# A static planner's stated durations and the order of a delta-rule mixer's projections, in a kernel of three blocks on one Trainium2 core

## The chip, the cores and the metric

The kernel runs on one core of one Trainium2 chip. The metric is the device time of one execution in microseconds. A core has five engines that run their own instruction streams in order and wait for each other by semaphores: TensorE (PE, matrix products and transposes), VectorE (DVE), ScalarE (ACT), GpSimd (POOL) and SyncE (SP, which here only issues DMAs). TensorE writes to PSUM, which has eight banks of 128 x 512 float32.

## The reference, cut to what matters

The sequence has 512 tokens of width 1024, in float32. Layer 0 is a dilated band attention with a memory attention and a SwiGLU of width 2816. Layer 1 is a gated delta-rule mixer (DeltaNet) with a memory attention and again a SwiGLU. A second block with three mixers of its own (gated linear attention, S5, sparse attention) follows. The change touches the order of work in layer 1's mixer, and the planner that orders everything. The mixer, cut:

```python
qkv, z, gate_in, q_mem = split(h @ w_in, ...)          # 3*768, 768, 24, 256 columns
q, k, v = split(silu(conv5(qkv)), 3)                   # 6 heads of 128
q, k = l2norm(q) * 128 ** -0.5, l2norm(k)
g, beta = -exp(a_log) * softplus(gate_in[..., 0] + dt_bias), sigmoid(gate_in[..., 1])
# forward and backward, per head, in chunks of tokens:
decay = exp(tril(g_i - g_j))                           # g: running sum in the chunk
a     = strict_tril(k_beta @ k.T * decay) + eye
u, w  = triangular_solve(a, [v * beta, k_beta * exp(g)])   # the inverse
intra = tril(q @ k.T * decay)
# then chunk by chunk a state S: v_new = u - w S; out = (q exp(g)) S + intra v_new; S = S exp(g_last) + ...
o = (o_fwd + o_bwd) normed * out_norm * silu(z)
out = concat([o, memory_attention(q_mem)]) @ w_out
```

## The kernel before

**Products in three passes.** Each float32 operand is split into a high and a low part (`wh`, `wl` for weights, `Xh`, `Xl` for activations), and `mm3` (lines 271 to 273) issues three matmuls into one bank: high by low, low by high, high by high. A projection of 128 columns over 512 tokens is eight `mm3` of 128x128 by 128x512. Weights come in pieces of 512 KB: `fetch` issues the DMA on SP into one of three raw buffers, `high` rounds the piece on ACT (line 243, two halves), `low` subtracts on DVE (line 262, two halves).

**The planner.** `Flow` builds the program by list scheduling. Each part of the work is a Python generator that yields an engine and a stated cost before it issues an instruction, or a wait for an event, or a request for a buffer (`get`, one of a counted set). `run` keeps a modelled clock per engine, picks the engine whose next step could start first, and among the steps of that engine that could start within `DELTA` = 0.1 us takes the one with the smallest `late`. The step then occupies its engine for its cost, and its result is ready at the end of it; a step on another engine can start `HOP` = 0.2 us after that. The result is a fixed order of instructions per engine. The costs do nothing else: no instruction waits for a planned time. Stated costs are `act(n)` = 0.1 + 0.00084 n (0.1 more with an accumulator or a per-partition scale), `dve(n)` = 0.07 + 0.00105 n, 0.65 us for an `mm3` of 512 columns and 0.33 us for one of 256 in most places, 0.68 us in `tok_proj`.

**The mixer.** In `deltanet` (line 1168) every head has threads `key`, `decays`, `query`, `value`, `gate`, `inverse`, two of `chain` (forward and backward), and `gate_out`.

- `key` takes the projection from its bank, convolves (ACT copy line 1313, DVE taps line 1322), normalises, transposes to `ktok` and `kTh`, multiplies `kk` (line 1392) and copies it to `kkn`.
- `decays` makes, for each direction d, a row broadcast `rowbc` (line 279), the decay `AT`, and from `kkn` and `AT` the matrix `Ln` (line 1424, DVE). It takes a bank of the set `px` for each d, and asks for the second one after d = 0 is done, which needs `kkn`.
- `query` multiplies `kq` (line 1447) and holds a `px` bank until `AT` of both directions is there.
- `inverse` waits for both `Ln` and then goes through six levels and a last half level: products and transposes on PE (`x`, lines 1508 and 1512), ACT copies (line 1519), products on PE (`y`, line 1533), DVE predicated copies (line 1537). At the end PE line 1553, DVE copies (line 1558) and ACT (line 1546) write `Uf`. Two inverses can be in flight.
- `chain` then walks over four chunks (lines 1580 to 1616), and each of the two chains of a head holds a `px` bank from its start to its end.
- `gate_out` norms, transposes and writes `oT`, which `splits` rounds for the output projection.

The banks are counted in sets: `mm` 2, `px` 3, `lv` 3. Other sets that bind here: `E` 2 (raw keys, values and gates), `qT` 1, `Ln`, `AT`, `qe`, `kd`, `k` 2 each. `projector` (line 1775) is the thread that issues the projections, in the order of a list, with `late` = 20, so that each `mm3` of it fills PE where nothing else is ready. The first four of the list run in two halves of 256 columns and on two lent banks. A projection holds its `mm` bank until its consumer has copied it out. The same list orders the DMAs and the splits of the weights.

**The list before** (`deltanet_weights`, line 1158): gates, then for heads 0, 1, 2 key, query, value, z; then the memory's two; then key, query, value of heads 3, 4, 5; then z of heads 3, 4, 5.

Of the kernel before, what the change touches and what calls it, by code (L numbers as in the profile page):

```python
# [35 lines left out]
S = 512  # L36
# [19 lines left out]
class Flow:  # L56
# [4 lines left out]


    HOP = 0.2

    def __init__(self, **sets):
        self.free = dict.fromkeys(("PE", "ACT", "DVE", "POOL", "DMA"), 0.0)
# [32 lines left out]
    def run(self):  # L99
        while self.threads:  # L100
            again = True
            while again:
                again = False
                for t in list(self.threads):
                    kind, *arg = t["req"]
                    value = None
                    if kind == "get" and any(self.sets[n] for n in arg):
                        value = min((n for n in arg if self.sets[n]), key=lambda n: min(self.sets[n])[0])
                        tok = min(self.sets[value])
                        self.sets[value].remove(tok)  # L110
                    elif kind == "two" and len(self.sets[arg[0]]) > 1:
                        for _ in range(2):
                            tok = min(self.sets[arg[0]])
                            self.sets[arg[0]].remove(tok)
                    elif kind == "wait" and all(e["tok"] for e in arg):
                        tok = max((e["tok"] for e in arg), key=lambda x: x[0])
                    elif kind == "move" and self.sets[arg[0]]:
                        src, dst = arg
                        tok = min(self.sets[src])
                        self.sets[src].remove(tok)  # L120
                        self.put(dst, tok)
                        tok = t["tok"]
                    elif kind == "late":
                        t["late"] = arg[0]
                        tok = t["tok"]
                    else:
                        continue
                    if tok[0] > t["tok"][0]:
                        t["tok"] = tok
                    self.step(t, value or tok)  # L130
                    again = True
            ops = []
            for t in self.threads:
                if t["req"][0] in self.free:
                    eng, cost, *after = t["req"]
                    ops.append((self.start(eng, after or [t["tok"]]), t))
            assert ops or not self.threads, ([(t["gen"].__name__, t["req"]) for t in self.threads], self.sets, self.free)
            if not ops:
                return
            s, t = min(ops, key=lambda x: x[0])  # L140
            s, t = min((x for x in ops if x[1]["req"][0] == t["req"][0] and x[0] <= s + DELTA), key=lambda x: x[1]["late"])
            eng, cost = t["req"][:2]
            self.free[eng] = s + cost
            t["tok"] = (s + cost, eng)
            self.step(t, t["tok"])
# [17 lines left out]
class K:  # L163
# [132 lines left out]
    def inputs(self, F, W, eX, eM, eF, pro):  # L296
# [93 lines left out]
        def memory():  # L390
            yield "late", 0.5
            for l in range(2):
                yield "wait", *eN[l]
                for c in range(2):
                    ev = W["mk"][l][c]
                    yield "wait", ev
                    yield "get", "mm"
                    p = self.psum("mm")
                    w = ev["W"]
                    for k in range(KT):  # L400
                        t = yield "PE", 0.33
                        self.mm3(p[:, :256], (w.h[:, k, :], w.l[:, k, :]), (M[l].h[:, k, :], M[l].l[:, k, :]),
                                 k == 0, k == KT - 1)
                    F.put("wsl", t)
                    F.add(evac(self.memK[l][:, c, :], p), 0.5, t)
                yield "wait", *W["mv"][l]
                for u in range(2):
                    yield "get", "mm"
                    p = self.psum("mm")
                    ts = slice(u * P, (u + 1) * P)  # L410
                    for k in range(KT):
                        w, kk = W["mv"][l][k // 4]["W"], k % 4
                        t = yield "PE", 0.33
                        self.mm3(p[:, :256], (M[l].h[:, k, ts], M[l].l[:, k, ts]), (w.h[:, kk, :], w.l[:, kk, :]),
                                 k == 0, k == KT - 1)
                    F.add(evac(self.memV[l][:, u, :], p, l == 1 and u == 1), 0.5, t)
                for _ in range(2):
                    F.put("wsl", t)
# [118 lines left out]
    def attention(self, F, W, eX, eM, eB, at, e2):  # L537
# [41 lines left out]
        def group(g):  # L579
# [37 lines left out]
            for i, t0 in enumerate((0, 64, 192, 320, 384)):  # L617
                yield "get", "mm"
                p = self.psum("mm")
                for k in range(KT):  # L620
                    w, kk = W2[k // 4]["W"], k % 4
                    t = yield "PE", 0.33
                    self.mm3(p[:, :256], (X.h[:, k, t0:t0 + P], X.l[:, k, t0:t0 + P]), (w.h[:, kk, :], w.l[:, kk, :]),
                             k == 0, k == KT - 1)
                F.add(copy_v(g, i, p[:, :256], r["t"][2][:, i, :], "mm"), g - 0.5, t)
# [394 lines left out]
    def out_ffn(self, F, i, W, gnext, groups, kev, before):  # L1020
# [57 lines left out]
        for part, (f0, f1) in enumerate(self.PARTS):  # L1078
# [22 lines left out]
            while f < nf:  # L1101
                fs = (f, f + 1) if part == 0 and f == 0 else (f,)
                banks = {}
                for hv in ((0, 256), (256, 512)) if len(fs) == 2 else ((0, 512),):
                    t0, t1 = hv
                    for u in range(t0 // P, t1 // P):
                        yield "wait", eX[u]
                    for f_ in fs:
                        for z in range(2):
                            ev = gu[part][f_][z]  # L1110
                            yield "wait", ev
                            if (f_, z) not in banks:
                                nm = yield "get", *self.ANY
                                banks[f_, z] = self.psum("bk"), nm
                            p = banks[f_, z][0]
                            for k in range(KT):
                                tk = yield "PE", 0.65 * (t1 - t0) / 512
                                self.mm3(p[:, t0:t1], (ev["W"].h[:, k, :], ev["W"].l[:, k, :]),
                                         (X.h[:, k, t0:t1], X.l[:, k, t0:t1]), k == 0, k == KT - 1)
                            if t1 == S:  # L1120
                                F.put("wsl", tk)
                        if t1 == S:
                            F.add(evac_gu(f_, (banks[f_, 0], banks[f_, 1], tk)))
                f += len(fs)
                if part == 0 and f == 4:
                    yield "DMA", 1.4
                    r["post"], _ = row("rowA", a["norm_ffn_post"][i])
                    yield "DMA", 1.4
                    r["gain"], _ = row("rowB", gnext)
                    r["ev"] = [F.event() for _ in range(4)]  # L1130
                    r["eX"] = [F.event() for _ in range(4)]
                    r["store"] = True
                    n4[:] = [0] * 4
# [24 lines left out]
    def deltanet_weights(self):  # L1158
# [2 lines left out]
        r = {n: [self.weight(w, 0, KT, z * 768 + h * P, P) for h in range(6)] for z, n in enumerate("qkvz")}  # L1161
        r["g"] = self.weight(w, 0, KT, 3072, P)
        r["m"] = [self.weight(w, 0, KT, 3096 + c * P, P) for c in range(2)]
        N = 3
        heads = [[r[n][h] for n in ("kqvz" if h < N else "kqv")] for h in range(6)]
        return r, [r["g"]] + sum(heads[:3], []) + r["m"] + sum(heads[3:], []) + r["z"][N:]

    def deltanet(self, F, wev, order, eX, res):

# [587 lines left out]
    def proj(self, F, ev, eX, m=P):  # L1757
# [7 lines left out]
        for t0, t1 in rngs:  # L1765
            yield "wait", *eX[t0 // P:t1 // P]
            for k in range(KT):
                t = yield "PE", 0.65 * (t1 - t0) / S
                self.mm3(p[:m, t0:t1], (W.h[:, k, :], W.l[:, k, :]), (X.h[:, k, t0:t1], X.l[:, k, t0:t1]),
                         k == 0, k == KT - 1)  # L1770
        F.put("wsl", t)
# [3 lines left out]
    def projector(self, F, items, eX, eP, late=20, haste=0):  # L1775
# [9 lines left out]
        def part(it, t0, t1):  # L1785
            W, m = it["W"], it["args"][4]
            yield "wait", *eX[t0 // P:t1 // P]
            for k in range(KT):
                t = yield "PE", 0.65 * (t1 - t0) / S
                self.mm3(it["p"][:m, t0:t1], (W.h[:, k, :], W.l[:, k, :]), (X.h[:, k, t0:t1], X.l[:, k, t0:t1]),  # L1790
                         k == 0, k == KT - 1)
            if t1 == S:
# [13 lines left out]
        for i, it in enumerate(items):  # L1806
# [13 lines left out]
            for u in range(4):  # L1820
# [3 lines left out]
                sl = slice(u * P, (u + 1) * P)  # L1824
                for k in range(KT):
                    W, kk = it[k // 4]["W"], k % 4
                    t = yield "PE", 0.33
                    self.mm3(p[:, :256], (X.h[:, k, sl], X.l[:, k, sl]), (W.h[:, kk, :], W.l[:, kk, :]),
                             k == 0, k == KT - 1)
                evac, late_ = it[0]["use"]["f"]  # L1830
# [392 lines left out]
    def s5(self, F, W, eX, open_, eY, uT):  # L2223
# [140 lines left out]
        def glu():  # L2364
# [14 lines left out]
            for c in range(2):  # L2379
                zs = []  # L2380
                for o in (2, 0):
# [1 line left out]
                    p = self.psum("lv", "glu")  # L2383
                    os_ = slice((o + c) * P, (o + c + 1) * P)
                    for k in range(2):
                        t = yield "PE", 0.65
                        self.mm3(p, (w.h[:, k, os_], w.l[:, k, os_]), yh[k], k == 0, k == 1)
                    zs.append((p, t))
                if c:
# [896 lines left out]
```

## Time and profile before

| what | value |
|---|---|
| time, median of 3 runs (lowest to highest) | 1768.99 us (1767.22 to 1770.46) |
| time of the profiled execution | 1771.96 us |
| its span, first to last instruction | 1770.2 us |
| mean granted clock of TensorE over the span | 0.99 of full speed |

The sum of a prediction is made against the profiled execution, 1771.96 us, of which 1.8 us lie around its span; it is 3.0 us over the median of the runs. Layer 1's mixer fills about 660 to 1020 us of the span.

### The profile page before, as it was taken

The page shows a single profiled execution, that of the slowest core. Times are in us where ns is not written, and L with a number is a line of the kernel's source. Part 1 is how long each engine was busy: PE and PEld are TensorE (multiplying, and loading weights), DVE is VectorE, ACT ScalarE, POOL GpSimd, SP SyncE. Part 2 cuts the span into 40 slices and gives each one's busy share as a digit, 9 for nine tenths or more (in the row PEclk, how much of TensorE's full clock was granted, in tenths as well). Part 3 has the DMA queues.
Part 4 walks back from the last instruction along what each step waited for, and adds up shares of the span by engine and source line. Part 5 has one row for each costly group of instructions (what it writes and reads, how often), then busy time and mean ns, then how long its engine had stood idle before and what let it go on. Part 6 is the DMA issues. An engine that isn't in the chain of part 4 may idle for free.

```text
span 1770.2 us, 30809 instructions
## 1 busy us (share of the span) xinstructions
PE 1718.8 (97%) x12391; PEld 1431.1 (81%) x12391; DVE 951.0 (54%) x1895; ACT 797.4 (45%) x1922; POOL 276.0 (16%) x440
## 2 busy tenths in 40 slices
PE   6999999999999999999999899999999999999999
PEld 5988679888888887787877778888888888888787
DVE  6333656323333378756765467464433468467573
ACT  5443635333222247657666455333222353345671
POOL 5200001000000020000000152375540033210000
PEclk8999999999999999999999999999999999999999
DMA  6513133333233333102010165344333253552012
GB/s 194 152 51 96 49 119 96 119 96 95 96 95 96 96 119 84 50 26 61 26 49 26 33 157 141 104 146 134 106 108 102 80 154 112 151 160 70 25 37 84
DMA packets 211983, 167.88 MB, mean 95 GB/s; under 512 B 21996, under 2 KB 183036, under 8 KB 211840
## 3 DMA queue, kind: packets, MB, share of 16 engines
q1 hardware_dynamic: 203808, 154.39, 29.6%
q0 software_dynamic: 4560, 9.42, 2.1%
q10 hardware_dynamic: 3472, 2.10, 0.4%
q8 instruction: 97, 1.59, 0.4%
q14 instruction: 46, 0.38, 0.1%
HBM read 152.23 MB, written 13.65 MB: 94 GB/s over the span
## 4 chain that ended last, share of the span: by engine, by line
PE 89%; DVE 6%; ACT 2%; issue 2%; DMA 1%; POOL 1%; ACTq 0%; SPq 0%; DVEq 0%; POOLq 0%
PE bk L271 23%; PE bk L272 23%; PE bk L273 23%; PE x L1508 1%; PE x L1512 1%; PE y L1533 1%; PE no L2740 1%; PE npT L2723 1%; DVE wl L262 1%; DVE hs L940 1%; PE chain L1588 1%; PE ns L2709 1%; PE hT L947 1%; PE ns L2707 1%; PE o L1608 1%
## 5 line engine op out<-in xcount | busy, mean ns | idle before, releaser
L262 DVE TENSOR_TENSOR wl<-raw,wh 128x512 fp32r<-128x512 f32 x450 | 314.7, 740 | 386.7 <-ACT wh L243 386.3
L243 ACT ACTIVATE wh<-raw 128x512 fp32r<-128x512 f32 x474 | 273.0, 622 | 532.9 <-PE bk L273 296.6
L271 PE MATMUL bk<-Xh,wl 128*128 128x512 f32 (+2 forms) x1312 | 494.6, 377 | 0.2 <-ACT Xh L949 0.2
L272 PE MATMUL bk<-Xl,wh 128*128 128x512 f32 (+2 forms) x1312 | 477.9, 364 | 0.5 <-DVE Xl L954 0.3
L273 PE MATMUL bk<-Xh,wh 128*128 128x512 f32 (+2 forms) x1312 | 478.0, 364 | 0.0
L271 PEld LDWEIGHTS bk<-Xh,wl 128*128 128x128 f32 (+1 forms) x1312 | 247.0, 188 | 40.1 <-issue 4.1
L273 PEld LDWEIGHTS bk<-Xh,wh 128*128 128x128 f32 (+1 forms) x1312 | 246.7, 188 | 39.8
L272 PEld LDWEIGHTS bk<-Xl,wh 128*128 128x128 f32 (+1 forms) x1312 | 247.3, 188 | 34.6 <-DVE Xl L954 0.9
L271 PE MATMUL bk<-wh,Xl 128*128 128x512 f32 (+1 forms) x424 | 152.6, 360 | 7.9 <-DVE Xl L794 3.7
L272 PE MATMUL bk<-wl,Xh 128*128 128x512 f32 (+1 forms) x424 | 145.4, 343 | 0.4 <-DVE wl L262 0.4
L273 PE MATMUL bk<-wh,Xh 128*128 128x512 f32 (+1 forms) x424 | 145.5, 343 | 0.0
L271 PE MATMUL bk<-wh,Al 128*128 128x512 f32 x352 | 139.7, 397 | 0.0
L272 PE MATMUL bk<-wl,Ah 128*128 128x512 f32 x352 | 139.5, 396 | 0.0
L273 PE MATMUL bk<-wh,Ah 128*128 128x512 f32 x352 | 138.6, 394 | 0.0
L919 POOL TENSOR_TENSOR nc<-ncm,nhalf 128x1 f32<-128x1 f32 x16 | 11.6, 726 | 666.8 <-DVE ncm L917 664.4
L271 PEld LDWEIGHTS bk<-wh,Xl 128*128 128x128 f32 x424 | 84.9, 200 | 19.2 <-DVE Xl L794 3.1
L1091 DVE TENSOR_TENSOR sg<-sg,bk 128x512 f32<-128x512 f32 x44 | 30.2, 688 | 124.4 <-PE bk L273 119.9
L272 PEld LDWEIGHTS bk<-wl,Xh 128*128 128x128 f32 x424 | 85.0, 201 | 7.7 <-DVE wl L262 1.1
L273 PEld LDWEIGHTS bk<-wh,Xh 128*128 128x128 f32 x424 | 84.6, 200 | 8.0
L271 PEld LDWEIGHTS bk<-wh,Al 128*128 128x128 f32 x352 | 66.0, 188 | 16.1
L273 PEld LDWEIGHTS bk<-wh,Ah 128*128 128x128 f32 x352 | 66.0, 188 | 16.1
L272 PEld LDWEIGHTS bk<-wl,Ah 128*128 128x128 f32 x352 | 66.1, 188 | 15.3
(577 smaller groups left out, 2590.9 us busy)
## 6 DMA issues: line engine op xcount, KB each, us to landing
raw<-in_ffn_w_gate_up_dram SPq DMA_DIRECT2D x88, 512.0 KB, 3.8
raw<-in_ffn_w_down_dram SPq DMA_DIRECT2D x44, 512.0 KB, 3.4
raw<-in_dn_w_in_dram SPq DMA_DIRECT2D x27, 512.0 KB, 3.8
raw<-in_att_w_in_dram SPq DMA_DIRECT2D x20, 512.0 KB, 3.9
raw<-in_w_in_dram SPq DMA_DIRECT2D x20, 512.0 KB, 3.7
raw<-in_mem_w_kv_dram SPq DMA_DIRECT2D x8, 512.0 KB, 3.5
raw<-in_att_w_out_dram SPq DMA_DIRECT2D x8, 512.0 KB, 3.3
xd<-x SPq DMA_DIRECT2D x8, 512.0 KB, 2.6
```

Of the source, the lines that this page charges most:

```text
L243: nc.scalar.activation(wh[:, sl], ev["raw"][:, sl], AF.Copy)
L262: eng.tensor_tensor(wl[:, sl], raw[:, sl], wh[:, sl].bitcast(F32), op=OP.subtract)
L271: mm(out, A[1], B[0], start=first, stop=False, **kw)
L272: mm(out, A[0], B[1], start=False, stop=False, **kw)
L273: mm(out, A[0], B[0], start=False, stop=last, **kw)
L940: nc.vector.scalar_tensor_tensor(hh[:, hv[i]], x[:, t, hv[i]], r2, r["gain"][:, hv[i]], op0=OP.mult, op1=OP.mult)
L947: nc.tensor.transpose(p[:, k * P:(k + 1) * P], hh[:, i * 512 + k * P:i * 512 + (k + 1) * P], self.ident)
L1091: nc.vector.tensor_tensor(sg, sg, pu, op=OP.mult)
L1508: nc.tensor.matmul(dn8(b[i])[at], lhsT, rhs, start=True, stop=True)
L1512: nc.tensor.transpose(b[d][:, o:o + P], U[:, d, 2 * n:2 * n + 2, :].rearrange("p c q -> p (c q)"), self.ident)
L1533: nc.tensor.matmul(dn8(ys[par])[HB[f], d, n, :], T[d][HB[par], n, f, :], xs[f][HB[par], d, n, :], start=True, stop=True)
L1588: nc.tensor.matmul(b[:, P:2 * P], Uf[:, d, c, :], rh, start=True, stop=True)
```

## The change

The planner's cost of each step on DVE is raised by 0.08 us and of each step on ACT by 0.07 us (`STEP`); the stated cost of an `mm3` goes from 0.65 to 0.682 us for 512 columns and from 0.33 to 0.36 us for 256. In the mixer's list each of the keys 1, 2 and 3 now stands ahead of the z of the head before it, and key 3 also ahead of the memory's two projections:

| list | order |
|---|---|
| before | g, k0 q0 v0 z0, k1 q1 v1 z1, k2 q2 v2 z2, m0 m1, k3 q3 v3, k4 q4 v4, k5 q5 v5, z3 z4 z5 |
| after | g, k0 q0 v0, k1 z0 q1 v1, k2 z1 q2 v2, k3 z2 m0 m1 q3 v3, k4 q4 v4, k5 q5 v5, z3 z4 z5 |

```diff
     HOP = 0.2
+    STEP = {"DVE": 0.08, "ACT": 0.07}
...
             eng, cost = t["req"][:2]
+            cost += self.STEP.get(eng, 0.0)
             self.free[eng] = s + cost
             t["tok"] = (s + cost, eng)
...
-                        t = yield "PE", 0.33
+                        t = yield "PE", 0.36
...
-                                tk = yield "PE", 0.65 * (t1 - t0) / 512
+                                tk = yield "PE", 0.682 * (t1 - t0) / 512
...
-        N = 3
-        heads = [[r[n][h] for n in ("kqvz" if h < N else "kqv")] for h in range(6)]
-        return r, [r["g"]] + sum(heads[:3], []) + r["m"] + sum(heads[3:], []) + r["z"][N:]
+
+        k, q, v, z = (r[n] for n in "kqvz")
+        order = [r["g"], k[0], q[0], v[0]]
+        for h in (1, 2, 3):
+            order += [k[h], z[h - 1]] + (r["m"] if h == 3 else []) + [q[h], v[h]]
+        return r, order + [k[4], q[4], v[4], k[5], q[5], v[5], z[3], z[4], z[5]]
...
-                t = yield "PE", 0.65 * (t1 - t0) / S
+                t = yield "PE", 0.682 * (t1 - t0) / S
```

The same two replacements of PE costs stand in `inputs`, `attention`, `out_ffn`, `proj`, `projector` and the second block's GLU. No instruction is added or taken away.

## Rows read from the trace of the kernel before

**Rows 1.** The page's first part: span, busy time and share of engines.
```profile
span 1770.2 us, 30809 instructions
...
PE 1718.8 (97%) x12391; PEld 1431.1 (81%) x12391; DVE 951.0 (54%) x1895; ACT 797.4 (45%) x1922; POOL 276.0 (16%) x440
```
**Rows 2.** Busy time in stretches; the first line names the columns.
```profile
core 0: us, PE busy (x) PEld busy (x) DVE busy (x) ACT busy (x) POOL busy (x), PEclk, DMA share, GB/s
...
180.00:240.00 60.00, 53.00 (x432) 39.53 (x431) 41.01 (x96) 33.40 (x109) 0.00 (x0) 0.98 0.11 36
240.00:640.00 400.00, 399.56 (x1856) 331.65 (x1856) 158.06 (x261) 131.54 (x253) 7.36 (x11) 1.00 0.34 103
...
660.00:1020.00 360.00, 344.01 (x4219) 283.38 (x4218) 233.31 (x499) 228.31 (x641) 22.86 (x25) 0.97 0.17 46
```
**Rows 3.** The same view of short stretches: one in attention, two in the mixer.
```profile
237.20:240.60 3.40, 3.40 (x10) 2.62 (x9) 1.08 (x2) 0.03 (x1) 0.00 (x0) 0.50 0.00 0
...
779.90:783.30 3.40, 2.93 (x15) 2.80 (x14) 2.78 (x7) 3.31 (x9) 0.00 (x0) 0.51 0.57 154
...
926.70:933.50 6.80, 6.26 (x90) 5.30 (x92) 1.99 (x4) 4.42 (x14) 0.00 (x0) 0.50 0.00 0
```
**Rows 4.** TensorE's waits, 640 to 1050: waiter <- releaser: total us, times, longest.
```profile
PE pk L1333 <- DVE kraw L1303: 3.6, 1, 3.6
PE chain L1588 <- DVE Uf L1558: 2.6, 3, 1.9
...
PE bk L271 <- DVE Xl L1693: 2.2, 1, 2.2
PE x L1508 <- DVE Ln L1424: 2.2, 1, 2.2
```
**Rows 5.** Groups by line and shape, DVE and ACT, 660 to 1020.
```profile
L262 DVE TENSOR_TENSOR wl<-raw,wh 128x512 fp32r<-128x512 f32 x54 | 34.8, 687 | 23.8 <-ACT wh L243 23.8
...
L1558 DVE COPY Uf<-y 64x128 f32<-64x128 f32 x24 | 6.9, 288 | 6.7 <-PE y L1553 6.3
...
L243 ACT ACTIVATE wh<-raw 128x512 fp32r<-128x512 f32 x54 | 31.1, 623 | 18.5 <-PE bk L273 18.2
```
**Rows 6.** Timeline of the end of head 1's inverse: start, duration, engine.
```profile
777.30 1.15 ACT L243 ACTIVATE wh<-raw 128x512 fp32r<-128x512 f32 x2 [0.43 <-PE bk L273]
...
777.97 1.29 DVE L262 TENSOR_TENSOR wl<-raw,wh 128x512 fp32r<-128x512 f32 x2 [4.01 <-ACT wh L243]
...
779.18 1.21 DVE L1558 COPY Uf<-y 64x128 f32<-64x128 f32 x4
...
779.60 0.46 PE L1588 MATMUL chain<-vtok,Uf 128*128 128x128 f32 x2 [1.93 <-DVE Uf L1558]
```
**Rows 7.** Timeline of TensorE: one matmul and its like three later, both sizes.
```profile
654.96 0.28 PE L271 MATMUL bk<-Xh,wl 128*128 128x256 f32 x1
...
655.31 0.28 PE L271 MATMUL bk<-Xh,wl 128*128 128x256 f32 x1
...
768.45 0.40 PE L271 MATMUL bk<-Xh,wl 128*128 128x512 f32 x1
...
769.14 0.40 PE L271 MATMUL bk<-Xh,wl 128*128 128x512 f32 x1
```
**Rows 8.** Timeline of TensorE: head 2's decays, kk, kq, its inverse's start (cut).
```profile
765.35 0.54 PE L279 MATMUL rowbc<-ident,gc 128*128 128x128 f32 x3
...
775.51 0.50 PE L1392 MATMUL kk<-kTh 128*128 128x128 f32 x3
...
781.09 0.63 PE L1447 MATMUL kq<-qTh,kTh 128*128 128x128 f32 x2
...
798.53 0.49 PE L279 MATMUL rowbc<-ident,gc 128*128 128x128 f32 x3
...
808.00 0.52 PE L1508 MATMUL x<-U,Ln 64*64 64x64 f32 x20
```

More of the change, by code (lines that the diff above doesn't have):

```diff
@@ L412, in memory @@
                         w, kk = W["mv"][l][k // 4]["W"], k % 4
-                        t = yield "PE", 0.33
+                        t = yield "PE", 0.36
                         self.mm3(p[:, :256], (M[l].h[:, k, ts], M[l].l[:, k, ts]), (w.h[:, kk, :], w.l[:, kk, :]),
@@ L621, in group @@
                     w, kk = W2[k // 4]["W"], k % 4
-                    t = yield "PE", 0.33
+                    t = yield "PE", 0.36
                     self.mm3(p[:, :256], (X.h[:, k, t0:t0 + P], X.l[:, k, t0:t0 + P]), (w.h[:, kk, :], w.l[:, kk, :]),
@@ L1788, in part @@
             for k in range(KT):
-                t = yield "PE", 0.65 * (t1 - t0) / S
+                t = yield "PE", 0.682 * (t1 - t0) / S
                 self.mm3(it["p"][:m, t0:t1], (W.h[:, k, :], W.l[:, k, :]), (X.h[:, k, t0:t1], X.l[:, k, t0:t1]),
@@ L1826, in projector @@
                     W, kk = it[k // 4]["W"], k % 4
-                    t = yield "PE", 0.33
+                    t = yield "PE", 0.36
                     self.mm3(p[:, :256], (X.h[:, k, sl], X.l[:, k, sl]), (W.h[:, kk, :], W.l[:, kk, :]),
@@ L2385, in glu @@
                     for k in range(2):
-                        t = yield "PE", 0.65
+                        t = yield "PE", 0.682
                         self.mm3(p, (w.h[:, k, os_], w.l[:, k, os_]), yh[k], k == 0, k == 1)
```

## Prediction

> **What bounds the kernel.** The page's first part comes first: TensorE is busy for 97% of the span, VectorE for 54%, ScalarE for 45% [rows 1]. A new order of the same instructions can therefore win only what TensorE loses in waits and at a lowered clock. The view by stretches tells where these are: between 240 and 640 us TensorE lacks 0.4 of 400 us, so a new order has nothing to win there; in layer 1's mixer, 660 to 1020, it lacks 360.00 - 344.01 = 16.0 us, and at the end of the attention, 180 to 240, 7.0 us [rows 2]. The same view over short stretches shows the granted clock at 0.50, the lower of its two levels (1.2 GHz for 2.4), right behind the larger waits: once after the attention, four times for 3.4 us in the mixer (one of them stands in the rows) and once for 6.8 us [rows 3]. At half speed the mixer loses half of 4 x 3.4 + 6.8 = 20.4 us, which is 10.2 us. The ceiling of a gain is then 16.0 + 10.2 in the mixer and 7.0 + 1.7 in the attention, 34.9 us in all.
>
> The view of waits names what TensorE waited for in the mixer: the first key's convolution (3.6 us), `Uf` at the start of the chains (2.6 us in three waits), head 4's `Ln` (2.2 us), and a split for the output projection at the very end (2.2 us) [rows 4]. These are 10.6 of the 16.0 us.
>
> **The stated durations.** For 512 elements the planner's VectorE cost was 0.07 + 512 x 0.00105 = 0.608 us and becomes 0.688; the recorded mean is 0.687 [rows 5]. ScalarE's was 0.530 and becomes 0.600; recorded 0.623 [rows 5]. `Uf`'s copy goes from 0.20 to 0.28; recorded 0.288 [rows 5]. So the new figures are the recorded durations. They are not the distance from one start to the next: two `wl` subtractions took 1.29 us together, so the second began 1.29 - 0.687 = 0.60 us after the first, and two `wh` copies took 1.15, a distance of 0.53 [rows 6]. Those are the old figures. The planner uses one number for both, and adds 0.2 us for the hop to another engine. The change thus makes results come 0.07 to 0.08 us later in the plan than in the plan before, and makes both engines busier than they are by some 13% on long steps (0.08 of 0.608, 0.07 of 0.530), more on short ones.
>
> On this the trace can be held against two statements of the Trainium skill. VectorE: DVE Perf Modes, section "The DRAIN you can't avoid", says that the next operation does not start before the former one's pipeline has run empty. By that rule the recorded duration would be the right occupancy too and the plan would become exact, which would favour the large gain below. The 0.60 us between two starts against 0.687 recorded [rows 5, 6] speaks for the other statement, Perfetto Trace Analysis, section "Optimizing Scalar/DVE Operations": part of the recorded latency overlaps the next instruction. By that one the new costs overstate occupancy, which favours the slower case below.
>
> The third edit makes TensorE's costs truer: three matmuls of 512 columns take 769.14 - 768.45 = 0.69 us (0.65 was stated, 0.682 will be), three of 256 take 0.35 (0.33, then 0.36) [rows 7].
>
> **What this moves.** The plan sees VectorE and ScalarE late, so it puts one more `mm3`, 0.69 us, ahead of many small TensorE steps that wait for them, as long as projections are left. In the case shown, the end of head 1's inverse, ScalarE got `wh` only when TensorE had released its buffer, VectorE did `wl` (1.29 us) ahead of the copies of `Uf`, and TensorE stood for 1.93 us before the chain [rows 6]. In the new plan four copies and two subtractions are 6 x 0.08 = 0.48 us later and two `wh` 0.14 us, together 0.62: about one `mm3` goes in front. That covers some 0.7 of the 1.93 us. The wait before head 3's chains, the same pair of lines, should go likewise: 1.4 us of the 2.6 [rows 4]. If the clock does not fall behind them, 2 x 1.7 us more come back [rows 3]. The bounds of this term are 0 and 2.6 + 3.4 = 6.0 us; I take 3.5, since it is nearer to a cover of one `mm3` each with one of the two falls of the clock avoided.
>
> Head 4's wait for `Ln`, 2.2 us, stands ahead of the long half-speed stretch, 6.8 us, worth 3.4 [rows 3, 4]. Key 4 keeps its place in the list, but what runs beside it changes. Bounds 0 and 5.6 us; I take the middle, 2.8.
>
> **The list.** A projection is 8 x 0.69 = 5.5 us of TensorE. Keys 1 and 2 come one place earlier, key 3 three places (16.6 us); z 0, z 1, z 2 and the memory's two come one place later; everything from q 3 on keeps its place. The DMAs of the pieces on SP, their `wh` on ScalarE and their `wl` on VectorE move with the list, the same number of each, so the queues carry no more. What is queued behind a key in its bank is the next projection: the key waits for one of two `E` buffers with one of two `mm` banks in hand, where z gave its bank back after one ScalarE and one VectorE step.
>
> What is gained is seen at head 2. The broadcast of its first direction ran at 765.35, `kk` at 775.51, `kq` at 781.09, the broadcast of the second direction only at 798.53, and the inverse began at 808.00 [rows 8]. From the code: the second broadcast needs a `px` bank, `decays` asks for it only after `kkn`, and by then head 1's two chains (their start is the last line of rows 6) and head 2's `kq` held all three. With key 2 a place or more ahead, `kk` comes 5.5 us earlier at least, near 770, and the second broadcast can run before the chains begin at 779.6. Head 2's inverse would then start some 20 us earlier, beside the end of head 1's. That in itself gives no time, because TensorE did projections meanwhile; it leaves those as fill for later. The gain is bounded by the waits not yet counted, 16.0 - 10.6 = 5.4 us, and by 0 below; I take 1.5, nearer to nothing, because those waits are short and spread.
>
> The first key's wait, 3.6 us, and the last split's, 2.2 [rows 4], I cost at no change: nothing was ready to fill the first (no bank was free for a further projection), and all projections are done at the second. Should the first move, it is by about one `wl` pair or z's steps, 1.3 us either way [rows 6].
>
> Elsewhere only the stated durations act. The attention's end has 7.0 us of waits and one fall of the clock [rows 2, 3]; bounds 0 and 8.7 us of gain, or as much as one `mm3` for each of some ten short waits, 7 us, of loss; I take a gain of 1.5, near nothing.
>
> **Sum.** 3.5 + 2.8 + 1.5 + 1.5 = 9.3 us less. From the profiled execution's 1771.96 us this gives 1762.7; the median of the runs stands 3.0 us lower, so 1768.99 - 9.3 = 1759.7 us is the prediction.
>
> **Rivals.**
>
> *Slower: the padded plan stretches the inverse.* An inverse visits TensorE 14 times (six levels and the half level, twice each). If one needless `mm3` stands before each visit, an inverse lasts 14 x 0.69 = 9.7 us longer. While projections are left this costs nothing; it decides from the point where the last pair of inverses runs and z 3 to z 5 are used up, for then nothing covers the end of the last head. 1768.99 + 9.7 = 1778.7 us. For it: the overstated occupancy [rows 5, 6], and the fact that heads 4 and 5 keep their places while work of heads 2 and 3 moves ahead of them. Against it: true latencies hold too, since the hop is part of them.
>
> *No change.* The waits are dealt anew but add up to as much, as 16.0 us of waits were left by a plan that had the strides right; key 1 sits in its bank for want of an `E` buffer and gains nothing; the long end from key 5 to the output projection is bound by its own latency. 1768.99, within 3.5 us either way.
>
> *Larger gain.* The pairs of inverses overlap as the list wants, the plan is close enough to keep TensorE fed, and all of the mixer's losses go but for the first key's wait and its clock (5.3), the last split's wait and its clock (3.9): 26.2 - 9.2 = 17 us, with the attention's 3 us 20 us. 1749 us. For it: all three keys arrive earlier and TensorE's costs become true [rows 7]. Against it: `px` and `E` are as few as before.
>
> **Chances.** Forecast (1753 to 1765.5) 0.37, larger gain 0.13, no change 0.22, slower 0.28. A change of 0.2%, 3.5 us, is about what a measurement of this kernel can tell from none. So faster 0.50, same 0.22, slower 0.28. Both signs hold much of the chance; the range of the likeliest case alone is 1753 to 1765.5. The range for 8 in 10 is 1747 to 1778: it leaves out the end of the large gain and that of the slower case.
>
> **What would show it.** As many instructions as before. The inverse of head 2 starts near 785 to 790 us instead of 808, with `rowbc` of its second direction ahead of head 1's chains; if it does not, the list's step is wrong. The waits of the chains for `Uf` fall to under 1.5 us and the stretches at clock 0.50 in the mixer from five to three or fewer; if the waits are as large at other lines, no change is right. If the mixer is longer and TensorE waits behind key 5, with projections used up, the padded plan is right. Between 240 and 640 us nothing should move by more than 1 us. What would make the forecast wrong is above all a new order with long waits at places that I can't see in the order before.

## The result, and the profile after

The changed kernel is slower: 1786.68 us, median of four runs (1784.56 to 1787.36), against 1769.72 us before in the same job. The ratio is 1.0096, 95% interval [1.0078, 1.0113]. A gain of 9.3 us was forecast; a loss of 17 us came. Single executions far slower than their like, at a clearly lower granted clock (2800.83 us at 0.59 in `f2_occupancy`, 1891.92 us at 0.847 in `g4_pe_mid_list`), are left out of every median and ratio below. The profiled execution took 1787.05 us with a span of 1785.3 us, 15.1 us over the span before [rows 1].

The first part of the profile's page of the kernel after, the counterpart of [rows 1]:

```profile
span 1785.3 us, 30812 instructions
...
PE 1716.7 (96%) x12391; PEld 1430.2 (80%) x12391; DVE 950.1 (53%) x1895; ACT 790.1 (44%) x1918; POOL 279.7 (16%) x440
```

TensorE executed as many matmuls, in 2.1 us less of busy time, so the 15 us are not longer work: it lacks 68.6 us of the span (length less busy time) for 51.4 before. To see where, I cut both spans into stages at the same matmul of the products in three passes, counted from the start. First the kernel before: the stretch with the output projection of the attention and its norms, the mixer, and the second block.

```profile
236.50:347.20 110.70, 110.27 (x585) 94.86 (x584) 54.04 (x95) 44.49 (x92) 5.74 (x8) 0.98 0.39 124
...
647.30:1019.20 371.90, 354.51 (x4308) 293.86 (x4307) 244.53 (x518) 233.59 (x654) 27.59 (x31) 0.97 0.18 50
...
1426.40:1770.20 343.80, 335.94 (x2842) 281.54 (x2840) 211.60 (x458) 165.37 (x425) 48.14 (x54) 1.00 0.35 99
```

The same stages of the kernel after (from, to, length, then busy time of each engine in the order of [rows 2]):

```profile
237.60:352.20 114.60, 112.23 (x586) 96.39 (x585) 54.04 (x95) 44.33 (x92) 6.79 (x8) 0.97 0.38 120
...
652.50:1026.40 373.90, 351.44 (x4307) 291.12 (x4307) 243.28 (x517) 233.18 (x656) 28.73 (x34) 0.98 0.18 51
...
1436.10:1785.30 349.20, 336.63 (x2841) 282.49 (x2840) 211.50 (x458) 165.34 (x426) 49.36 (x55) 0.99 0.35 98
```

The stages grow by 3.9, 2.0 and 5.4 us; ahead of the first the attention has grown by 1.1, behind the mixer its output projection and the norms by 2.4, and the two long SwiGLU stretches by 0.3 together. That is the 15.1 us. Less than a seventh of it lies in the mixer, the only place where the list of projections changed. What TensorE lacks is 2.4 us for 0.4 in the first stage, 22.5 for 17.4 in the mixer, 12.6 for 7.9 in the second block.

The stretches of [rows 2] of the kernel after:

```profile
180.00:240.00 60.00, 50.22 (x424) 38.28 (x423) 41.86 (x97) 33.08 (x109) 0.00 (x0) 0.99 0.11 36
240.00:640.00 400.00, 397.63 (x1834) 330.07 (x1833) 153.28 (x252) 129.03 (x248) 7.88 (x10) 0.99 0.34 103
660.00:1020.00 360.00, 341.11 (x4246) 281.92 (x4244) 233.43 (x501) 226.11 (x638) 18.71 (x20) 0.98 0.17 47
```

The second line was not to move by more than 1 us. TensorE now lacks 2.4 us there for 0.4, and a stretch of 3.4 us ran at a clock of 0.50, which is worth 1.7 us. The timeline of the kernel after at 283 us shows the place. It lies in a norm, whose chain runs over VectorE, GpSimd and TensorE:

```profile
282.96 0.75 DVE L925 SCALAR_TENSOR_TENSOR x<-y,nc,x 128x512 f32<-128x512 f32 x1 [0.44 <-POOL nc L921]
283.63 1.41 DVE L942 SCALAR_TENSOR_TENSOR hs<-x,nc,rowB 128x512 f32<-128x512 f32 x2
...
284.43 0.44 PE L949 MATMUL hT<-ident,hs 128*128 128x128 f32 x2 [1.65 <-DVE hs L942]
```

TensorE stands 1.65 us for the normed rows `hs`; at 286.0 the granted clock falls to 0.50 (view of short stretches, the counterpart of [rows 3], with the longest one of the mixer):

```profile
286.00:289.40 3.40, 3.40 (x18) 3.40 (x17) 2.96 (x7) 1.06 (x3) 1.53 (x1) 0.50 0.50 144
...
688.80:699.00 10.20, 5.03 (x18) 4.10 (x19) 6.06 (x12) 7.61 (x30) 1.12 (x1) 0.50 0.11 34
```

Norms lose elsewhere too: TensorE waits for `hs` 1.9 us for 0.4 in the first stage, 2.1 for 0.5 behind the mixer, and in the second block, before (first two lines) and after:

```profile
PE hT L947 <- DVE hs L940: 1.0, 1, 1.0
PE gs L2095 <- POOL ge L2074: 0.6, 1, 0.6
...
PE hT L949 <- DVE hs L942: 2.3, 3, 1.3
PE gs L2100 <- POOL ge L2079: 1.8, 2, 1.6
PE ncsT L2666 <- ACT sqt L2660: 1.3, 1, 1.3
PE glu L273 <- DVE wl L264: 1.0, 1, 1.0
```

No single wait carries the loss of the second block. The waits of TensorE of the kernel after, 640 to 1050, the counterpart of [rows 4]:

```profile
PE pkT L1338 <- DVE ktok L1371: 6.0, 2, 3.8
PE bk L273 <- DVE Xl L1698: 4.7, 2, 2.5
PE pk L1338 <- DVE kraw L1308: 2.6, 1, 2.6
PE y L1538 <- ACT xT L1524: 1.8, 4, 1.0
PE x L1513 <- DVE U L1542: 1.8, 3, 0.7
...
PE rowbc L281 <- DVE gc L1278: 1.6, 1, 1.6
```

The waits that the forecast named did shrink: over the whole span those for `Uf` from VectorE went from 2.6 to 0.5 us and those for `Ln` from 2.2 to 0.5. New ones stand elsewhere: 6.0 us for `ktok`, a key's normalised rows (3.8 of them at the first key), and 4.7 for 2.2 us for the last splits ahead of the output projection. A sign that the prediction named came as well: the second `rowbc` of head 2 runs at 789.35, ahead of head 1's chains at 793.27.

### The profile page after: what moved, and what is told of

It is laid out like the page before. It is cut to its first block, busy times and chain, and to the rows that moved or that the text cites. A ratio compares the mean times of both kernels' runs of the same rounds, so it can differ in the third digit from the quotient of the medians.

```text
span 1785.3 us, 30812 instructions
## 1 busy us (share of the span) xinstructions
PE 1716.7 (96%) x12391; PEld 1430.2 (80%) x12391; DVE 950.1 (53%) x1895; ACT 790.1 (44%) x1918; POOL 279.7 (16%) x440
## 4 chain that ended last, share of the span: by engine, by line
PE 87%; DVE 5%; ACT 3%; POOL 2%; issue 1%; DMA 1%; ACTq 0%; SPq 0%; DVEq 0%; POOLq 0%
PE bk L273 23%; PE bk L274 22%; PE bk L275 22%; PE x L1513 1%; PE x L1517 1%; PE y L1538 1%; PE no L2745 1%; PE npT L2728 1%; ACT wh L245 1%; PE ns L2714 1%; DVE x L925 1%; POOL wl L264 1%; PE ns L2712 1%; PE o L1613 1%; DVE wl L264 1%
```

## The experiments

Every run compares with the kernel before on the same chip. "Mixer" and "second block" are the lengths of the stages in the profiled execution, cut as above (before: 371.9 and 343.9 us).

### The three parts, one by one

The list alone (`e1_list`), the raise per step alone (`e2_step`), TensorE's costs alone (`e3_pe`), and a change that has nothing to do with the trace, the hop's figure (`e4_hop`):

```diff
# e1_list: deltanet_weights as in the change
# e2_step
+    STEP = {"DVE": 0.08, "ACT": 0.07}
...
+            cost += self.STEP.get(eng, 0.0)
# e3_pe
-                        t = yield "PE", 0.33
+                        t = yield "PE", 0.36
...
-                                tk = yield "PE", 0.65 * (t1 - t0) / 512
+                                tk = yield "PE", 0.682 * (t1 - t0) / 512
# e4_hop
-    HOP = 0.2
+    HOP = 0.21
```

> The kernel before with the new list of projections alone; all stated durations as before. If the list is what costs, the mixer takes the blame: 1780 us or more, with the first key's wait as long as in the changed kernel (two stalls of 2.8 and 4.1 us, 10.2 us at half clock). If the durations are what costs, the list alone gives 1765 to 1770 us (my forecast's own gain of the list was 1.5 us), head 2's inverse starts before 808 us, and nothing ahead of 640 us moves.

> The kernel before with 0.08 us on each step of VectorE and 0.07 on each of ScalarE alone. If padded durations are what costs, this one has most of the 17 us: 1780 to 1787 us, with losses in the attention's end, the norm chains and the second block. If it is the list or TensorE's costs, 1766 to 1773 us. If any new deal of the order costs about as much, 1775 us or so, as for the next two.

> The kernel before with 0.682 and 0.36 us for a product in three passes alone. They are closer to the rows than 0.65 and 0.33 were, so if a truer plan is a better one: 1762 to 1768 us. If any new deal costs, 1772 to 1778 us.

> The kernel before with the hop between engines at 0.21 us for 0.20: no claim of truth in it, a nudge that deals the order anew. If the loss comes from what the new figures mean, 1767 to 1772 us. If the order before was a lucky or picked one and any new deal loses, 1773 us or more.

| run | median us | ratio [95%] | mixer | second block |
|---|---|---|---|---|
| e1_list | 1769.45 | 0.9993 [0.9982, 1.0004] | 371.4 | 343.5 |
| e2_step | 1796.36 | 1.0149 [1.0132, 1.0166] | 379.7 | 350.6 |
| e3_pe | 1786.29 | 1.0093 [1.0078, 1.0108] | 369.7 | 356.4 |
| e4_hop | 1778.89 | 1.0050 [1.0033, 1.0067] | 371.4 | 348.1 |

The list does what it was to do in the plan and is worth nothing that these runs can tell. The second `rowbc` of head 2 and the start of its inverse in `e1_list`; they stood at 798.53 and 808.00 [rows 8]:

```profile
779.87 0.60 PE L279 MATMUL rowbc<-ident,gc 128*128 128x128 f32 x4
...
784.80 0.88 PE L1510 MATMUL x<-U,Ln 64*64 64x64 f32 x32
```

The inverse begins 23 us earlier and the mixer ends at nearly the same time. The waits show why. TensorE's waits in `e1_list`, 640 to 1050:

```profile
PE poT L1335 <- ACT otok L1644: 3.7, 1, 3.7
...
PE pq L1335 <- DVE qTh L1305: 1.8, 1, 1.8
...
PE chain L1590 <- DVE Uf L1560: 0.9, 2, 0.7
```

The list alone, without the raise per step, takes the wait for `Uf` from 2.6 to 0.9 us and that for `Ln` from 2.2 to nothing. In their place TensorE stands 3.7 us for `otok`, the output rows of a head near the mixer's end (1.6 before), and 1.8 for `qTh`; it lacks 17.1 us in the mixer, for 17.4. `e3_pe` is alike: no wait for `Uf`, 0.3 us for `Ln`, 17.3 lacking.

Each set of costs loses by itself, more than either expectation allowed, and so does a hop that is 0.01 us longer.

### Results later, or engines fuller

The raise per step does two things in the plan. `f1_latency` keeps only the later result, `f2_occupancy` only the fuller engine:

```diff
# f1_latency
-            t["tok"] = (s + cost, eng)
+            t["tok"] = (s + cost + self.STEP.get(eng, 0.0), eng)
# f2_occupancy
-            self.free[eng] = s + cost
+            self.free[eng] = s + cost + self.STEP.get(eng, 0.0)
```

> The kernel before with the 0.08 and 0.07 us added to the time at which a result is ready, while the engine is free again at the old cost. If the padding costs because it overstates how long the engines are occupied, this form does not, and lands with the nudge of the hop: 1772 to 1782 us. If later results are what costs (fill put ahead of steps that could go), it has the whole loss of the padded durations: 1790 to 1798 us.

> The other half: the engine is occupied 0.08 or 0.07 us longer, the result ready at the old time. If overstated occupancy costs: 1788 to 1798 us, with VectorE and ScalarE work put late in the mixer and in the second block. If later results cost: 1770 to 1780 us, the size of a nudge.

Measured: 1781.6 us, 1.0067 [1.0052, 1.0082], and 1779.71 us, 1.0062 [1.0041, 1.0083]. Both lose the same, in the attention and its norms (5.1 and 4.4 us by the end of that first stage) and in the second block (349.5 and 349.8). Neither lengthens the mixer (368.5 and 371.1). So the loss can't be put down to the overstated occupancy: the half without it loses as much.

### Nudges without a meaning

If false costs were the cause, a hop or a `DELTA` that is a little off should do less than a cost that is 13% off.

```diff
# n1_hop19
-    HOP = 0.2
+    HOP = 0.19
# n2_delta
-DELTA = 0.1
+DELTA = 0.11
# n3_hop201
-    HOP = 0.2
+    HOP = 0.201
```

> A nudge the other way, hop 0.19 us for 0.20. If any new deal of the order loses: 1774 to 1785 us. If it was the direction, results later, that lost 9 us at 0.21: 1762 to 1770 us.

> A nudge of a figure that states no duration: the window in which the planner lets the more urgent step go first is 0.11 us for 0.10. If any new deal loses: 1774 to 1785 us. If stated durations matter and deals do not: 1767 to 1772 us.

> The smallest nudge: hop 0.201 us for 0.200. No duration on the chip is that well known. If the order before is one good draw among many, this loses 5 to 15 us too: 1774 to 1785 us. If the loss grows with the size of the change, 1768 to 1772 us.

| run | median us | ratio [95%] | mixer | second block |
|---|---|---|---|---|
| n1_hop19 | 1793.92 | 1.0138 [1.0121, 1.0155] | 378.3 | 358.2 |
| n2_delta | 1779.60 | 1.0058 [1.0041, 1.0075] | 371.6 | 347.9 |
| n3_hop201 | 1775.84 | 1.0029 [1.0017, 1.0041] | 371.4 | 351.8 |

A hop that is one nanosecond longer costs 0.29%, and the second block is where it is lost. The stretch of `n3_hop201` that answers to the last stage above:

```profile
1424.40:1776.20 351.80, 341.38 (x2841) 285.38 (x2839) 212.71 (x458) 166.21 (x425) 48.13 (x54) 0.98 0.34 97
```

TensorE lacks 10.4 us for 7.9, and the clock fell twice where it did not fall before:

```profile
1706.80:1713.60 6.80, 6.80 (x48) 6.02 (x47) 5.35 (x13) 3.92 (x16) 0.00 (x0) 0.50 0.02 6
1720.40:1723.80 3.40, 3.23 (x13) 2.83 (x14) 2.42 (x6) 2.11 (x10) 0.00 (x0) 0.50 0.00 0
```

TensorE was busy for 10.0 us of them, which at half speed is a loss of 5.0. With the 2.5 us of waits this is 7.5 of the 7.9 us by which the stage is longer. The matmuls are the same, their order is not: by the names of the tiles, 510 of TensorE's 2840 places in this stage hold another matmul than before.

### The new costs in one stage at a time

All new costs, but in force only while one part of the program is planned: layer 0 (`h1_front`), layer 1, with the new list (`h2_middle`), the second block (`h3_second`). `TRUE` maps TensorE's old costs to the new (in `h3_second` it also takes one step of three transposes, stated at 0.33 us, to 0.36, which the change leaves alone).

```diff
+            more = self.STEP.get(eng, 0.0) if self.on else 0.0
+            if self.on and eng == "PE":
+                cost = self.TRUE.get(cost, cost)
+            cost += more
...
+                F.on = True    # h2; False in h1 and h3
                 eK, eP, close = self.deltanet(F, W1, order1, eX, res)
...
+                F.on = False   # h2 and h1; True in h3
                 st.enter_context(self.second(F, W3, eX, res, out))
```

> All the new durations, but only in the plan of layer 0 (attention, its output projection and SwiGLU); the mixer and all behind it planned with the durations and the list of before. From where the changed kernel's losses stand in its trace, this part should cost 4 to 6 us: 1774 to 1776 us. If a new order ahead deals the rest anew as well, 1779 us or more.

> The new list and the new durations in the plan of layer 1 alone (mixer, output projection, SwiGLU). By the changed kernel's trace 3 to 6 us: 1773 to 1776 us. If my forecast of the mixer was right and only the rest went wrong, 1762 to 1767 us.

> The new durations in the plan of the second block alone. By the changed kernel's trace 4 to 7 us: 1774 to 1777 us. If the second block's loss came from what lay ahead of it, 1768 to 1771 us.

Measured: 1774.64 us, 1.0026 [1.0017, 1.0036]; 1776.48 us, 1.0037 [1.0023, 1.0051]; 1775.15 us, 1.0030 [1.0020, 1.0040]. The three losses add to 0.93%, for 0.96% of the whole change. Each part of the program loses about a third of it with the other parts planned as before. The mixer is 373.9 us in `h2_middle`, the second block 350.0 in `h3_second`, where TensorE waits for `ge` (1.6 us), `sqt` (1.3) and `wl` (1.0) as in the kernel after.

### In layer 1 alone: which costs, with and without the list

The same switch, on in layer 1 only: the later result alone (`g1_lat_mid`; with the list `g2_lat_mid_list`), or TensorE's costs alone (`g3_pe_mid`; with the list `g4_pe_mid_list`).

```diff
# g1, g2
+    STEP = {"DVE": 0.08, "ACT": 0.07}
+    TRUE = {}
...
+            t["tok"] = (s + cost + more, eng)
# g3, g4
+    STEP = {}
+    TRUE = {0.33: 0.36, 0.65: 0.682, 0.325: 0.341}
```

> Layer 1 alone planned with results 0.08 and 0.07 us later (engines free at the old cost), list and TensorE's costs of before. Used everywhere, this form made the stretch from the mixer to its SwiGLU some 3 us shorter and lost elsewhere. If layers can be dealt apart: 1764 to 1768 us, faster than before. If that gain hung on the order ahead of it: 1768 to 1774 us.

> The same with the new list. If list and later results add up (about -2 and -3 us in the traces): 1762 to 1767 us. If each pair is a deal of its own: anywhere from 1764 to 1780 us, with no relation to the parts.

> Layer 1 alone planned with 0.682 and 0.36 us for a product in three passes, which the rows bear out. Used everywhere, the costs made this stretch some 2 us shorter. If a truer plan helps where it is not undone elsewhere: 1765 to 1768 us. If not: 1769 us or more.

> The same with the new list: 1763 to 1767 us if the list's earlier inverse and truer costs add up, my forecast's mechanism without the padding; 1770 us or more if the pair is just another deal.

| run | median us | ratio [95%] | mixer |
|---|---|---|---|
| g1_lat_mid | 1768.44 | 0.9992 [0.9982, 1.0001] | 369.2 |
| g2_lat_mid_list | 1771.58 | 1.0006 [0.9997, 1.0015] | 374.0 |
| g3_pe_mid | 1766.31 | 0.9979 [0.9969, 0.9988] | 368.0 |
| g4_pe_mid_list | 1762.54 | 0.9957 [0.9941, 0.9973] | 364.1 |

The last one beats both kernels, by 0.43% over the kernel before, and its mixer is 7.8 us shorter. TensorE's costs and the list gain more together than the sum of their parts (0.21% and 0.07%), though the intervals leave room for a plain sum. The later result gains nothing clear of noise, alone or with the list, where the expectations had held a gain possible for both.

### Is it the padding, and is the gain a draw?

Two questions stayed: whether the raise per step (the padding) alone undoes that gain in the mixer (`i1_step_mid_list`), and whether the gain outlives another small change of TensorE's cost (`i2_pe70_mid_list`).

```diff
# i1: against g4
-    STEP = {}
-    TRUE = {0.33: 0.36, 0.65: 0.682, 0.325: 0.341}
+    STEP = {"DVE": 0.08, "ACT": 0.07}
+    TRUE = {}
# i2: against g4
-    TRUE = {0.33: 0.36, 0.65: 0.682, 0.325: 0.341}
+    TRUE = {0.33: 0.36, 0.65: 0.7, 0.325: 0.35}
```

> The new list and, in layer 1 alone (mixer to SwiGLU), the 0.08 and 0.07 us more per step of VectorE and ScalarE; TensorE's stated costs stay at 0.65 and 0.33. Theory A (the padding is what hurts the mixer, truer TensorE costs help it): no gain, 1770 to 1780 us, with the mixer at 372 us or more, where list and truer TensorE costs gave 364. Theory B (the padding hurts only together with the raised TensorE costs, each alone is harmless): 1762 to 1768 us. Theory C (each order is a draw of its own and no term has a size): any of the two, so this run alone can't support it.

> As list and truer TensorE costs in layer 1 alone, which ran at 0.9957 of the kernel before, but with 0.70 us for an mm3 of 512 columns in place of 0.682 (0.35 for half of one); recorded are 0.69 and 0.35. Theory A (the gain comes from TensorE costs nearer to the trace): the gain stays, 1760 to 1766 us, the mixer at 362 to 368 us. Theory C (that run was one lucky draw among orders): it is gone or turns, 1768 to 1778 us, since the order changes as much as by any other nudge.

Measured: `i1` 1783.41 us, 1.0084 [1.0065, 1.0102], mixer 379.4 us; `i2` 1761.01 us, 0.9955 [0.9938, 0.9971], mixer 364.5 us. The padding in place of TensorE's costs turns the gain into a loss, a larger one than expected, and the gain stays at 0.70, in an order of its own (by the tiles' names the two mixers part at the 91st matmul). So Theory A stands, Theory B falls with `i1`, and Theory C does not fit `i2`. `h2_middle` above says the same of the padding: it is `g4_pe_mid_list` with the raise per step added and nothing else, and its mixer lasts 373.9 us for 364.1. The mixer of `g4_pe_mid_list`, as a stretch:

```profile
646.40:1010.50 364.10, 349.22 (x4309) 287.77 (x4308) 244.04 (x518) 232.11 (x654) 26.61 (x30) 0.98 0.18 52
```

and that of `i1_step_mid_list`, which differs from it in the stated costs alone:

```profile
646.10:1025.50 379.40, 352.28 (x4308) 291.64 (x4307) 243.56 (x518) 232.35 (x655) 26.98 (x31) 0.97 0.18 50
```

TensorE lacks 14.9 us in the first and 27.1 in the second: waits are 12.2 of the 15.3 us between them. The clock is little of it. TensorE was granted 0.50 for 13.6 us in the first and 19.5 in the second, but was busy for only 8.6 and 10.1 of these, so half speed cost 4.3 and 5.0 us, 0.7 more. The last 2.4 us are not accounted for. The timeline shows the waits best at one place, the few microseconds behind the first key's transpose `pk`. In `g4_pe_mid_list` ScalarE takes the third `craw`, which empties a projection's bank, before it turns to the key:

```profile
682.02 0.57 ACT L1322 ACTIVATE craw<-bk 128x512 f32<-128x512 f32 x1
...
682.97 0.78 PE L278 MATMUL bk<-Xh,wl 128*128 128x512 f32 x1
...
683.52 1.16 ACT L1423 ACTIVATE AT<-rowbc,ngc 128x128 f32<-128x128 f32 x4
```

In `i1_step_mid_list` the same `craw` stands behind the key's sums of squares and five other steps:

```profile
685.29 0.28 ACT L1351 ACTIVATE sqacc<-pk 128x128 f32<-128x128 f32 x1 [1.34 <-PE pk L1342]
...
687.80 0.67 ACT L1310 ACTIVATE sqt<-hn 128x512 f32<-128x512 f32 x1
688.32 0.63 ACT L1322 ACTIVATE craw<-bk 128x512 f32<-128x512 f32 x1
...
689.08 1.08 PE L1342 MATMUL pkT<-ident,ktok 128*128 128x128 f32 x4 [3.83 <-DVE ktok L1375]
689.82 0.78 PE L278 MATMUL bk<-Xh,wl 128*128 128x512 f32 x1
```

No projection stands ahead of `pkT` in TensorE's order, and it stands 3.83 us. The clock is low around both places, in `i1_step_mid_list` (first line) for three times as long, but there TensorE had less to do:

```profile
681.70:691.90 10.20, 3.91 (x15) 3.17 (x16) 7.15 (x15) 6.64 (x24) 1.12 (x1) 0.50 0.19 52
...
682.30:685.70 3.40, 3.40 (x13) 2.82 (x12) 3.37 (x7) 3.38 (x15) 1.34 (x1) 0.50 0.53 140
```

That the bank is what was missing follows from the code, not from a row: the next projection comes right after that `craw` in both kernels. The kernel after has the same order: `craw` at 694.30, `pkT` at 695.05 after 3.82 us, within 10.2 us at the lower clock (688.8 to 699.0, shown above).

## Why the prediction was wrong

**What bounds the kernel: right in the main.** Time is TensorE's work, plus its waits, plus half of the time that it was busy at the lower clock. The mixer's length less the last two is 345.1 us before, 345.7 after, 344.9 in `g4`, 347.2 in `i1`, and between 342.7 and 347.4 in all twenty kernels, whose mixers last 364.1 to 379.7 us. So waits and clock carry most of a difference, and some 2 us stay unexplained. The forecast took half of the whole time at the lower clock, 10.2 us, beside all of the waits. TensorE was busy for 18.8 of those 20.4 us, so the clock was worth 9.4 and the rest was counted twice.

**The steps that failed. First: "Elsewhere only the stated durations act".** I put it at a gain of 1.5 us, with bounds for the attention's end alone. The rest of the program went without a price. The term, forecast at −1.5, came out at +13.1 of the 15.1 us: 5.0 up to 347 us (1.1 of them in the attention), 2.4 behind the mixer, 5.4 in the second block, 0.3 in the SwiGLU stretches. That between 240 and 640 us "a new order has nothing to win there" was true, and I read it as if nothing could happen there. A stage that loses 0.4 us in 110 can only get worse. `h1_front` and `h3_second` show that the new costs lose there with the mixer's plan as it was (0.26% and 0.30%).

Nor is it the falseness of the costs alone. The nudges, none of which says more or less of the trace than the figures before, lose 0.29 to 1.38%, and in all ten kernels that planned the second block with some other figure it is longer, by 4.0 to 14.3 us. For this block the order before is at the short end of its neighbours. How it came to be there no run shows.

**Second, the mixer: a wait that closes was booked as time.** The mixer was forecast at −7.8 us and came out at +2.0. `Uf`: forecast −3.5 with its clock, the wait fell by 2.1 us. `Ln`: forecast −2.8 with its clock, the wait fell by 1.7. The lower clock in the mixer: from 20.4 us to some 17, five stretches to three as was said, and TensorE was busy for 11.5 of them for 18.8, worth 3.6 us. But the credit to the raise per step is not borne out, since the list alone and TensorE's costs alone close the same waits and TensorE lacks as much as before (17.1 and 17.3 us for 17.4). The list: forecast −1.5, measured nothing alone. What I missed most is the first key: "I cost at no change". The waits for `pk`, `ktok` and the gates' sums went from 3.6 to 2.6 + 6.0 + 1.6 = 10.2 us (8.0 of them at the first key), and the last split's from 2.2 to 4.7. I had named the mechanism, a projection that holds its bank while its consumer waits, and gave it no place and no price.

**Which edit does what in the mixer.** Of the kernels that plan it with TensorE's truer costs and no padding, all four have a shorter mixer (364.1, 364.5, 368.0, 369.7 us); of those with the whole padding all four a longer one (373.9, 374.0, 379.4, 379.7); seven that leave its costs alone, pad only the occupancy, or have the longer hop or the wider `DELTA` lie at 371.1 to 372.4, and one with a shorter hop at 378.3. These are fewer orders than kernels: by the tiles' names `e3_pe` and `g3_pe_mid` have the same mixer, and that of `h2_middle` differs from the kernel after's in 34 of 4306 places. So a gain of 7.8 us in the mixer is there (`g4_pe_mid_list`), from the list with TensorE's costs, and with the padding it is gone. That it is the forecast's figure is luck: the edit that was to bring it is left out, and waits that the forecast did not name remain (3.7 us for `otok`, 3.1 for `vTh`). The prediction had the edits the other way round: it drew the gain from the raise per step and gave TensorE's costs no term.

**The rivals.** "No change" named what the list and TensorE's costs did in the mixer when each ran alone: the waits were dealt anew and added up to as much. The slower one had the right sign, and for the mixer the right edit, the raise per step; its reason and its place are not borne out. The overstated occupancy alone leaves the mixer at 371.1 us, and the inverses' own waits (for `xT` and `U`) went from 1.7 to 3.6 us, not up by 9.7. Of the two statements of the Trainium skill, the one under which the plan "would become exact" and gain is not borne out: the whole raise loses in every run. VectorE: DVE Perf Modes, section "The DRAIN you can't avoid", would have the recorded duration as the right occupancy, but the same section adds that a next operation which is not held starts earlier, so it does not stand against the other statement as the prediction had it; the 0.60 us between two starts [rows 6] stays the better reading. But `f1_latency`, which has the later result with the right occupancy, loses 0.67% too, so a truer model of these two engines isn't by itself a faster order.

**What stays open.** That a shorter mixer follows from truer TensorE costs rests on three orders against three, and `f1_latency` and `g1_lat_mid` have short ones (368.5 and 369.2 us) without them; the chain from a 0.032 us higher cost to the order with `craw` in front was read at one place only. Neither half of the padding lengthened the mixer alone with the list before (368.5 to 371.1 us), the later result with the new list did (374.0); why was not settled. Why the new costs open just those waits in the norms and the second block was not followed through the plan. A hundred random nudges, which would give the spread of such orders, were not run.

## What to carry to other kernels

When a static order is planned from stated costs, a change of one figure can deal the whole program anew: price every stage, and price a stage with nothing left to win as a loss. Do not book a wait as won because the edit closes it: look where the next one opens, and sum what the bottleneck lacks. Measure the spread with a few nudges without a meaning (here a hop 0.001 to 0.01 us off moved the time by 0.3 to 1.4%) before reading a gain or a loss of that size as the effect of an edit. Then confine the new figures to the stage that they were meant for: here the list and TensorE's costs, in layer 1 alone, give 0.9957 and 0.9955, where the whole change gave 1.0096.

## What the runs showed that was not expected

The clock can cost more than the waits: in `n3_hop201`, where a hop is one nanosecond longer, TensorE's waits in the second block grew by 2.5 us and its time at half speed cost 5.0. And time at the lower clock is no measure of the loss by itself. Around the first key of the kernel after TensorE was granted 0.50 for 10.2 us, but it stood for half of them and was busy for 5.0, so the clock cost 2.5 us there and the waits more.
